# Delta rule in 128-token chunks, its steps emitted between dense products, in a two-block network on one core

## Chip, cores and metric

The kernel runs on one core of a Trainium2 chip. The metric is device time in microseconds (us) of one execution, lower is better. Each time below is from the profiler's record of one execution or from timed runs of the whole kernel.

## What is computed

A two-layer network on 256 latent and 256 context tokens (width 1024) is followed by a second block of two layers on the 256 latent tokens. Only the second block's mixer is touched. It runs a gated delta rule over 8 heads of width 128 beside a sliding-window attention, and gates and sums the two. The reference does the delta rule in chunks of 64 tokens:

```python
def gated_delta_rule_chunked(q, k, v, g, beta):          # C = 64
    gc = cumsum(g) in each chunk
    decay = exp(where(tri_incl, gc[i] - gc[j], -inf))
    L = where(tri_strict, (k * beta) @ k.T * decay, 0)
    A = L + eye(C)
    u, w = solve(A, [v * beta, k * beta * exp(gc)])      # unit lower triangular
    qk = (q @ k.T) * decay
    def step(S, ...):
        v_new = u - w @ S
        o = (q * exp(gc)) @ S + qk @ v_new
        S = S * exp(g_last) + (k * exp(g_last - gc)).T @ v_new
```

The chunk length is a choice of the algorithm: with chunks of 128 the same outputs come from two chunks instead of four.

## The kernel before

All dense products split each float32 operand into a high and a low part and add three products (lines L189 to L191, `mm3`). Weights come in tiles of 512 KB: the SP queue loads `raw` (L177), ScalarE casts `whi` (L181), and VectorE or, for one tile in `pool_every`, GpSimd subtracts `wlo` (L183). Four buffers of each kind run ahead of TensorE.

`mixer2` writes the work of one mixer in program order; a scheduler then fixes the order on each engine by that order and by its own estimates of readiness. On the chip each engine runs its list in order. `Delta` holds the delta rule. Heads go in pairs `pr` (0 to 3); a pair has four blocks `u` (2 heads x 2 halves of 128 tokens).

- `first_keys`, `conv_silu`: projection, short convolution and silu of keys, queries and values, mixed with the dense products.
- `gates`: decay sums (L1672, L1676), written to DRAM so that `rows` can broadcast them.
- `keys`: transposes (L1738), the decay table `W` (L1754 to L1756), the links `LT` = k k^T times `W`, in 64x64 chunks (`chunks`, L1640), written to DRAM.
- `inverse`: 16x16 diagonal blocks are inverted on GpSimd in 15 dependent steps (L1777, L1779), and come back through DRAM as `inv`.
- `levels`: the 16-blocks are joined to 32 and to 64 with small products (L1640), two pairs at a time, and `wT` is made (L1816).
- `queries` and `values`: the table q k^T times decay, again in `chunks`, and the scaled values in `kf`.
- `recur`: four chunk steps (`tb`, `ch`); in each, for two groups `g` of four heads, R·kf (L1861) and wT·S (L1863) are added into one bank, k^T·vk makes the state update (L1871), and W·vt (L1873) and q·S (L1875) are added into the output bank.
- `turn`: transposes of the result (L1904) and their split.

The mixer emits them as whole calls: `keys` for all pairs, `inverse`, `queries`, `levels`, `values`, the z product (512 columns at a time), `recur`, then the gates `yb`, the attention's output product, the gates `ga`, `turn`. A float32 product is two instructions on TensorE: a listing of the order counts products, the trace counts instructions.

Of the kernel before, what the change touches and what calls it, by code (L numbers as in the profile page):

```python
# [19 lines left out]
P = 128  # L20
# [8 lines left out]
def _consts():  # L29
# [67 lines left out]
class Net:  # L97
# [184 lines left out]
    def setup(self):  # L282
# [6 lines left out]
        self.half = self.t(self.cp, [P, 16], tag="half")  # L289
# [989 lines left out]
    def setup2(self, cp):  # L1279
# [6 lines left out]
                      for nm, src, w in (("sgq", "swa_q_norm", 64), ("sgk", "swa_k_norm", 64), ("ssink", "swa_sinks", 16),  # L1286
                                         ("alog", "dn_a_log", 8), ("dtb", "dn_dt_bias", 8))} for l in range(2)]
# [51 lines left out]
    def mixer2(self, x, M, l):  # L1339
# [8 lines left out]
        def gates(dst, c0):  # L1348
            for fb in range(4):
                for _, pa in self.fm_pair(h, 256, w, c0 + fb * 256):  # L1350
                    nc.scalar.activation(dst[:, 2 * fb:2 * fb + 2], pa, AF.Tanh, scale=0.5)

        with pool("mx") as op, ExitStack() as ds:
# [7 lines left out]
            with pool("sw") as ap, pool("inv", side="right") as vp:  # L1361
# [16 lines left out]
                next(swa)  # L1378
                next(swa)
                next(swa)  # L1380
                for pr in range(4):
                    dn.keys(pr)
                dn.inverse(vp)
                dn.queries(0)
                dn.queries(1)
                dn.queries(2)
                dn.queries(3)
                for prs in ((0, 1), (2, 3)):
                    dn.levels(vp, prs)
                next(swa)  # L1390
                dn.values(0)
                next(swa)
                dn.values(1)
                next(swa)
                dn.values(2)
                dn.values(3)
                self.pool_every = 4
# [5 lines left out]
            gain = self.bcast_rows(dp, I["dn_norm_2"][l], P, "dgain")  # L1403
            nc.vector.tensor_scalar(gain, gain, 0.5, None, ALU.mult)
            for hf in range(2):
                def ev_z(tb, pa, hf=hf):
                    g = gz[tb][:, hf * 512:hf * 512 + 512].rearrange("p (h d) -> p h d", d=P)
# [3 lines left out]
                    nc.gpsimd.tensor_tensor(g, g, gain.unsqueeze(1).to_broadcast([P, 4, P]), ALU.mult)  # L1411
                self.proj_tm(h, TBS, w, Z + hf * 512, 512, ev_z)
            with pool("rec") as rp:
                ys = dn.recur(rp, gz)
                gates(yb, GB)
                ws = I["w_swa_out_2"][l]
                with pool("ys", side="right") as yp:
                    ysh, ysl = (self.t(yp, [P, 8, 256], F32R, tag=nm) for nm in ("ysh", "ysl"))
                    for k in (0, 4):
                        for s in (slice(0, P), slice(P, 256)):  # L1420
                            self.split(ysh[:, k:k + 4, s], ysl[:, k:k + 4, s], yT[:, k:k + 4, s])
                    for j in range(4):
                        for _, pa in self.fm_pair(self.flat(ysh, ysl), 256, ws, j * 256):
                            c = yb[:, 2 * j:2 * j + 2]
# [178 lines left out]
class Delta:  # L1603
# [127 lines left out]
    def keys(self, pr):  # L1731
        net, nc, u3, u4 = self.net, self.nc, self.u3, self.u4
        kf, kT, W, LT = self.kf[pr], self.kT[pr], self.W[pr], self.LT[pr]
        if pr > 1:
            self.conv_silu(1024, pr, kf)
# [206 lines left out]
```

## Time and profile before

| | us |
|---|---|
| median of 3 runs | 2421.25 (2411.98 to 2422.31) |
| profiled execution, device time | 2422.13 |
| its span, first to last instruction | 2420.2 |
| TensorE busy in the span | 2305.9 |
| VectorE / ScalarE / GpSimd busy | 1613.3 / 1063.9 / 756.3 |
| mean granted TensorE clock | 0.980 |

How to read it: the first delta stage runs at about 1335 to 1600 us (mixer of layer 0), the second at about 1890 to 2170 us (layer 1). PE is TensorE, DVE VectorE, ACT ScalarE, POOL GpSimd, SP the DMA queue. A timeline row has start, duration, engine, line, operation, out<-in, tile rows*columns, moving shape, count, and in brackets the idle time before it. Matmuls overlap, so what one costs is read from the start of one row to the start of the next. A window row has the stretch, its length, the busy time of PE, PE weight loads, DVE, ACT and POOL with instruction counts, the granted clock (1 is 2.4 GHz, 0.5 is 1.2 GHz), the DMA share and GB/s.

### The profile page before, as it was taken

To read this page: it belongs to the slowest core of one execution; us is meant where nothing else is said; L and a number is where in the kernel's file an instruction comes from. 1 tells how busy PE (TensorE), PEld (TensorE's weight loads), DVE (VectorE), ACT (ScalarE), POOL (GpSimd) and SP (SyncE) were. 2 spreads that over 40 slices of the span, in tenths; PEclk is the share of its full clock that TensorE was granted. 3 is DMA by queue.
4 is the path that set the end of the run, shared out by engine and by line. 5 is a ranking of instruction groups with operands and counts; after the bars stand their busy time and mean duration, and the time that the engine had idled before them with its cause. 6 is when DMAs were issued, how large, how long until landed. Compare 5 with 4: busy or idle time off the path is not lost.

```text
span 2420.2 us, 41624 instructions
## 1 busy us (share of the span) xinstructions
PE 2305.9 (95%) x16388; PEld 2017.7 (83%) x16388; DVE 1613.3 (67%) x2607; ACT 1063.9 (44%) x1748; POOL 756.3 (31%) x545
## 2 busy tenths in 40 slices
PE   6989989999999999988999999999999999999999
PEld 5767667777778788888998888799998887789999
DVE  2677858776566947488647886358766887448773
ACT  3555434332234533345445654245445564345443
POOL 1454421111013122123444662123224572114111
PEclk8989999999999999999999999999999899999999
DMA  7433335476666647477755543255655543245554
GB/s 240 148 105 106 126 111 164 154 227 211 203 203 190 202 154 244 133 242 227 233 180 155 160 115 107 70 157 159 190 183 159 163 120 103 74 139 174 167 183 140
DMA packets 348585, 394.64 MB, mean 163 GB/s; under 512 B 38269, under 2 KB 290093, under 8 KB 346341
## 3 DMA queue, kind: packets, MB, share of 16 engines
q1 hardware_dynamic: 346212, 391.86, 52.5%
q8 instruction: 128, 2.10, 0.4%
q14 instruction: 69, 0.56, 0.1%
q10 hardware_dynamic: 2176, 0.13, 0.1%
HBM read 389.27 MB, written 2.65 MB: 162 GB/s over the span
## 4 chain that ended last, share of the span: by engine, by line
PE 76%; DVE 11%; DMA 6%; issue 3%; POOL 2%; ACT 1%; SPq 1%; DVEq 0%; POOLq 0%; ACTq 0%
PE acc L191 21%; PE acc L190 21%; PE acc L189 21%; DMA mraw<-in_w_ada_dram 2%; DVE macc L383 2%; DVE wlo L183 1%; PE rc L1640 1%; DVE nt L619 1%; DVE hTl L621 1%; PE sm L1873 1%; PE rc L1861 1%; DMA mbig<-in_mod_w_dram 1%; DMA raw<-in_even_w_in_dram 1%; PE sm L1875 1%; PE rc L1863 1%
## 5 line engine op out<-in xcount | busy, mean ns | idle before, releaser
L181 ACT CAST whi<-raw 128x1024 fp32r<-128x1024 f32 (+2 forms) x536 | 552.5, 1033 | 603.1 <-PE acc L190 416.6
L183 POOL TENSOR_TENSOR wlo<-raw,whi 128x1024 fp32r<-128x1024 f32 (+1 forms) x168 | 411.8, 2451 | 1091.3 <-ACT whi L181 1006.7
L189 PE MATMUL acc<-hTh,whi 128*128 128x256 f32 (+2 forms) x2256 | 690.3, 308 | 14.4 <-DVE nu L601 7.9
L190 PE MATMUL acc<-hTl,whi 128*128 128x256 f32 (+2 forms) x2256 | 694.9, 308 | 7.9 <-DVE hTl L621 7.9
L191 PE MATMUL acc<-hTh,wlo 128*128 128x256 f32 (+2 forms) x2256 | 693.8, 308 | 0.7 <-DVE wlo L183 0.7
L183 DVE TENSOR_TENSOR wlo<-raw,whi 128x1024 fp32r<-128x1024 f32 (+1 forms) x368 | 481.0, 1308 | 306.2 <-ACT whi L181 299.8
L189 PEld LDWEIGHTS acc<-hTh,whi 128*128 128x128 f32 x2256 | 429.7, 191 | 46.6 <-issue 12.5
L190 PEld LDWEIGHTS acc<-hTl,whi 128*128 128x128 f32 x2256 | 430.0, 191 | 31.8 <-DVE hTl L621 10.2
L191 PEld LDWEIGHTS acc<-hTh,wlo 128*128 128x128 f32 x2256 | 429.9, 191 | 23.4 <-issue 2.0
L383 DVE SCALAR_TENSOR_TENSOR macc<-mraw,sil,macc 128x512 f32<-128x512 f32 x280 | 247.7, 894 | 82.2 <-DMA mraw<-in_w_ada_dram 43.0
L190 PE MATMUL acc<-hidl,whi 128*128 128x256 f32 (+1 forms) x704 | 218.1, 310 | 0.0
L191 PE MATMUL acc<-hidh,wlo 128*128 128x256 f32 (+1 forms) x704 | 217.7, 310 | 0.0
L189 PE MATMUL acc<-hidh,whi 128*128 128x256 f32 (+1 forms) x704 | 217.6, 310 | 0.0
L189 PE MATMUL acc<-whi,hTh 128*128 128x512 f32 (+2 forms) x496 | 182.4, 370 | 7.5 <-DVE pre L1708 2.8
L190 PE MATMUL acc<-wlo,hTh 128*128 128x512 f32 (+2 forms) x496 | 180.2, 364 | 2.7 <-POOL wlo L183 2.6
L191 PE MATMUL acc<-whi,hTl 128*128 128x512 f32 (+2 forms) x496 | 175.9, 366 | 2.9 <-DVE hTl L621 2.2
L189 PEld LDWEIGHTS acc<-hidh,whi 128*128 128x128 f32 x704 | 132.2, 188 | 9.7 <-issue 1.7
L191 PEld LDWEIGHTS acc<-hidh,wlo 128*128 128x128 f32 x704 | 132.6, 188 | 7.9
L190 PEld LDWEIGHTS acc<-hidl,whi 128*128 128x128 f32 x704 | 132.6, 188 | 7.9
L189 PEld LDWEIGHTS acc<-whi,hTh 128*128 128x128 f32 x496 | 95.1, 192 | 31.3 <-issue 8.4
L191 PEld LDWEIGHTS acc<-whi,hTl 128*128 128x128 f32 x496 | 93.6, 191 | 20.4 <-DVE hTl L621 4.5
L190 PEld LDWEIGHTS acc<-wlo,hTh 128*128 128x128 f32 x496 | 94.9, 191 | 18.0 <-POOL wlo L183 3.1
(531 smaller groups left out, 3829.1 us busy)
## 6 DMA issues: line engine op xcount, KB each, us to landing
raw<-in_w_in_dram SPq DMA_DIRECT2D x112, 512.0 KB
mraw<-in_w_ada_dram SPq DMA_DIRECT2D x192, 256.0 KB
raw<-in_ffn_w_in_dram SPq DMA_DIRECT2D x88, 512.0 KB
raw<-in_w_up_dram SPq DMA_DIRECT2D x88, 512.0 KB
mraw<-in_mod_w_dram SPq DMA_DIRECT2D x96, 256.0 KB
raw<-in_odd_w_in_dram SPq DMA_DIRECT2D x48, 512.0 KB
raw<-in_ffn_w_out_dram SPq DMA_DIRECT2D x40, 512.0 KB
raw<-in_w_down_dram SPq DMA_DIRECT2D x40, 512.0 KB
```

The source lines that it names most:

```text
L181: nc.scalar.copy(hi, raw)
L183: eng.tensor_tensor(lo, raw, hi.bitcast(F32), ALU.subtract)
L189: mm(out, lhsT=ah, rhs=bh, start=start, stop=False)
L190: mm(out, lhsT=ah, rhs=bl, start=False, stop=False)
L191: last = mm(out, lhsT=al, rhs=bh, start=False, stop=stop)
L383: nc.vector.scalar_tensor_tensor(accs[g, m], raw, v[:, k:k + 1], accs[g, m], ALU.mult, ALU.add)
L619: nc.vector.scalar_tensor_tensor(t, x[:, k], a, self.nrs[:, m * 256:m * 256 + 256], ALU.mult, ALU.mult)
L621: nc.vector.scalar_tensor_tensor(lo[:, k, c], t, b, hi[:, k, c].bitcast(F32), ALU.add, ALU.subtract)
L1640: self.nc.tensor.matmul(out[s, u * 64:u * 64 + 64], lhsT=l(u, s), rhs=r(u, s), start=True, stop=True)
L1861: mm(pv[r, s], lhsT=self.R[pr][r, u], rhs=self.kf[pr][r, u], start=True, stop=first)
L1863: mm(pv[r, s], lhsT=self.wT[pr][:, u, r], rhs=S[g][:, i], start=False, stop=True)
L1873: mm(po[g][r, s], lhsT=self.W[pr][r, u], rhs=vt[g][r, i], start=True, stop=first)
```

## The change

Chunks become 128 tokens long, so `W`, `LT` and `R` are 128x128 blocks and the recurrence has two steps in place of four. The products of links and queries are whole 128x128 blocks (`blocks`). `levels` gets one more join, from 64 to 128: the upper 64-block and lower 64-block are inverted as before and their lower-left corner is filled by two more products, which lie in one quarter of the array (`mm`); it works on all four pairs at once with eight `yield` points. `recur` loses the state scaling. `mixer2` calls these steps one by one between convolutions, z products (now 256 columns at a time), gates and the attention's output; `turn` now stands ahead of the last gate piece. The gain of `dn_norm` is loaded early, once.

```diff
-    c["d_min"] = np.where(r6 <= q6, 0.0, NEG).astype(np.float32)
-    c["tri"] = f(same & (r <= q))
-    c["blk"] = f(same)
+    c["d_min"] = np.where(r <= q, 0.0, NEG).astype(np.float32)
+    c["tri"] = f(r <= q)
...
                 sq(0, 0)
                 self.proj_tm(h, TBS, w, 0, 272, ev_k, rows=kab)
+                dn.gates()
                 sq(512, 0)
-                dn.gates()
                 heads = self.swa_heads(ap, sraw, l)
                 swa = self.swa(ap, sraw, heads, yT)
+                dn.keys(0)
+                dn.conv_silu(1024, 2, dn.kf[2])
                 next(swa)
+                dn.links(0)
+                dn.keys(1)
...
+                dn.links(3)
                 dn.inverse(vp)
                 dn.queries(0)
+                dn.conv_silu(0, 2, dn.q[2])
+                next(swa)
...
+                lev = dn.levels(lp)
+                next(lev)
+                dn.first_values(3)
+                dn.values(2)
                 self.pool_every = 4
+                next(lev)
+                z(0)
+                dn.values(3)
+                for f in (lambda: z(1), lambda: z(2), lambda: z(3), lambda: gate(yb, GB, 0), lambda: gate(yb, GB, 1)):
+                    next(lev)
+                    f()
+                for _ in lev:
+                    pass
...
+                next(rec)
+                gate(yb, GB, 3)
+                for j in range(4):
+                    next(rec, None)
+                    for _, pa in self.fm_pair(self.flat(ysh, ysl), 256, ws, j * 256):
...
+                for j in range(3):
+                    gate(ga, GA, j)
                 yd = dn.turn(ys)
+                gate(ga, GA, 3)
...
+    def blocks(self, out, l, r):
+
+        for u in range(4):
+            self.nc.tensor.matmul(out[:, u * P:u * P + P], lhsT=l[:, u], rhs=r[:, u], start=True, stop=True)
+        return self.u3(out)
...
+    def links(self, pr):
+
+        net, nc, kf, LT, W = self.net, self.nc, self.kf[pr], self.LT[pr], self.W[pr]
+        nc.vector.tensor_tensor(LT, self.blocks(net.rc(), kf, kf), W, ALU.mult)
+        nc.sync.dma_start(self.ldram[:, pr * 512:pr * 512 + 512], LT.rearrange("p u t -> p (u t)"))
...
+        def mm(pr, rows, l, r):
+
+            out = bank(pr)
+            for u in range(4):
+                nc.tensor.matmul(out[rows, u * 64:u * 64 + 64], lhsT=l(u), rhs=r(u), start=True, stop=True)
+            return self.uc(out)[rows]
...
+        up, low = halves
         for b in (16, 32):
             for pr in prs:
+                nc.vector.tensor_tensor(Y[pr], lt4(pr), lv(f"lev{b}"), ALU.mult)
+            yield
+            for pr in prs:
+                if b < 32:
+                    nc.vector.tensor_tensor(Tm[pr], Tm[pr], mm4(pr, R[pr], Y[pr]), ALU.subtract)
+                else:
+                    nc.vector.tensor_tensor(Tm[pr][up], Tm[pr][up], mm(pr, up, lambda u: R[pr][up, u], lambda u: Y[pr][up, u]), ALU.subtract)
+            yield
+            for pr in prs:
+                nc.vector.tensor_tensor(R[pr], R[pr], mm4(pr, Y[pr], R[pr]), ALU.subtract)
...
+            nc.scalar.copy(Y[pr][low], mm(pr, low, lambda u: LT[pr][up, u, low], lambda u: Tm[pr][up, u]))
+        yield
+        for pr in prs:
+            for s in halves:
+                nc.gpsimd.tensor_copy(F[pr][s, :, s], R[pr][s])
+            nc.vector.tensor_scalar(F[pr][up, :, low], mm(pr, up, lambda u: Y[pr][low, u], lambda u: R[pr][low, u]), -1.0, None, ALU.mult)
+        yield
...
+                for i, pr, u, s in hds[g]:
+                    mm(pv[:, s], lhsT=self.R[pr][:, u], rhs=self.kf[pr][:, u], start=True, stop=tb == 0)
+                    if tb:
+                        mm(pv[:, s], lhsT=self.wT[pr][:, u], rhs=S[g][:, i], start=False, stop=True)
...
+            yield
+            if tb == 0:
+                for g in range(2):
+                    px = net.rc()
+                    for i, pr, u, s in hds[g]:
+                        mm(px[:, s], lhsT=self.kT[pr][:, u], rhs=vk[g][:, i], start=True, stop=True)
+                    nc.vector.tensor_copy(S[g], self.u3(px))
```

The order of instructions on TensorE at three places of layer 0's mixer follows (rows: line, operation, out<-in, output rows x columns, products). The first is the recurrence; before, in its second chunk step (`acc` rows are dense gate products):

```order
L190 MATMUL acc_15068<-hTl_10417,whi_15058 128x256
L191 MATMUL acc_15068<-hTh_10416,wlo_15059 128x256
L1871 MATMUL rc_14712<-vk_2526_14685,kT_2116_12240 128x128 x2
L1871 MATMUL rc_14712<-vk_2526_14685,kT_2117_12241 128x128 x2
L1873 MATMUL sm_14687<-vt_2524_14683,W_2128_12252 64x128 x2
L1873 MATMUL sm_14687<-vt_2524_14683,W_2129_12253 64x128 x2
L1861 MATMUL rc_14722<-kf_2110_12234,R_2134_12258 64x128
L1863 MATMUL rc_14722<-S_2521_14680,wT_2118_12242 64x128
```

Products there have 64 output rows, and R·kf alternates with wT·S. In the changed kernel the corresponding step takes whole blocks, both head groups at once:

```order
L190 MATMUL acc_15059<-hTh_10420,wlo_15056 128x256
L1923 MATMUL rc_15109<-vk_2566_15031,kT_2115_12241 128x128 x2
L1923 MATMUL rc_15109<-vk_2566_15031,kT_2116_12242 128x128 x2
L1923 MATMUL rc_15115<-vk_2567_15032,kT_2117_12243 128x128 x2
L1923 MATMUL rc_15115<-vk_2567_15032,kT_2118_12244 128x128 x2
L1928 MATMUL sm_15121<-vt_2564_15029,W_2127_12253 128x128 x2
L1928 MATMUL sm_15121<-vt_2564_15029,W_2128_12254 128x128 x2
L1928 MATMUL sm_15122<-vt_2565_15030,W_2129_12255 128x128 x2
L1928 MATMUL sm_15122<-vt_2565_15030,W_2130_12256 128x128 x2
L188 MATMUL acc_15171<-ysh_15017,whi_15161 128x256
```

It stands between two runs of 48 dense instructions each, and so does every step of the new recurrence. The second place is the levels; before, two pairs at a time, with attention and value work close behind:

```order
L1640 MATMUL rc_13816<-T_2376_13748,LT_2130_12254 64x64 x8
L1640 MATMUL rc_13826<-T_2377_13749,LT_2131_12255 64x64 x8
L1544 MATMUL mod_14322<-spT_14308,sraw_2179_12485 64x256 x2
L1544 MATMUL mod_14322<-spT_14309,sraw_2180_12486 64x256 x2
L1844 MATMUL sm_14401<-k_ident_79,tmp_14328 128x128 x4
L1844 MATMUL sm_14480<-k_ident_79,tmp_14407 128x128 x4
```

In the changed kernel all four pairs follow each other, and the new one-quarter products (L1835) come behind:

```order
L1679 MATMUL sm_14705<-R_2453_14143,Y_2449_14139 64x64 x8
L1679 MATMUL rc_14715<-R_2454_14144,Y_2450_14140 64x64 x8
L1679 MATMUL sm_14725<-R_2455_14145,Y_2451_14141 64x64 x8
L1835 MATMUL rc_14735<-T_2444_14134,LT_2131_12257 64x64 x4
L188 MATMUL acc_14771<-hTh_10420,whi_14761 128x256
L189 MATMUL acc_14771<-hTl_10421,whi_14761 128x256
L1835 MATMUL sm_14741<-T_2445_14135,LT_2132_12258 64x64 x4
```

Each level's stage now has 16 or 32 products at a time, with dense products between most stages. The third place is `turn`; before, its 16 transposes stand together, right behind the last gate product:

```order
L191 MATMUL acc_15640<-hTh_10416,wlo_15637 128x256
L1904 MATMUL sm_15698<-k_ident_79,pre_14780 128x128 x4
L1904 MATMUL sm_15707<-k_ident_79,pre_14794 128x128 x4
L1904 MATMUL sm_15716<-k_ident_79,vt_2560_14906 128x128 x4
L1904 MATMUL sm_15725<-k_ident_79,vt_2565_14920 128x128 x4
L189 MATMUL acc_15755<-kT_2655_15690,whi_15745 128x256
```

In the changed kernel the first eight stand ahead of 45 dense instructions of the last gate piece, and the other eight near its end:

```order
L190 MATMUL acc_15717<-hTh_10420,wlo_15714 128x256
L1955 MATMUL sm_15687<-k_ident_79,vt_2612_15325 128x128 x4
L1955 MATMUL sm_15696<-k_ident_79,vt_2617_15339 128x128 x4
L188 MATMUL acc_15717<-hTh_10420,whi_15713 128x256
L189 MATMUL acc_15717<-hTl_10421,whi_15713 128x256
```

So dense work now lies between the two halves of the transposes. Over both mixers, TensorE goes from whole-array work to products on part of the array 92 times before and 61 times in the changed kernel, counted in the two orders from the decay sums on.

## Rows read from the trace of the kernel before

**Rows 1.** The page: busy time, share of the span and instructions of each engine.
```profile
PE 2305.9 (95%) x16388; PEld 2017.7 (83%) x16388; DVE 1613.3 (67%) x2607; ACT 1063.9 (44%) x1748; POOL 756.3 (31%) x545
```

**Rows 2.** Busy time by stretch: keys to levels, recurrence, a feed-forward stretch.
```profile
1335.00:1490.00 155.00, 146.05 (x1394) 127.96 (x1393) 127.80 (x275) 83.46 (x178) 90.02 (x75) 1.00 0.47 128
1490.00:1570.00 80.00, 80.00 (x552) 60.74 (x551) 30.62 (x55) 25.30 (x37) 11.04 (x6) 1.00 0.24 74
...
1700.00:1850.00 150.00, 150.00 (x1270) 150.00 (x1269) 96.24 (x119) 68.42 (x84) 39.80 (x20) 1.00 0.61 187
```

**Rows 3.** Waits of PE, 1335 to 1620 us: total, times, longest.
```profile
PE sm L1904 <- DVE q L168: 3.6, 1, 3.6
...
PE rc L1640 <- DVE T L1799: 1.3, 1, 1.3
```

**Rows 4.** The same view, 1890 to 2180 us.
```profile
PE sm L1904 <- DVE q L168: 2.4, 1, 2.4
```

**Rows 5.** Groups by line, PE: the recurrence's products (busy us, mean ns).
```profile
L1873 PE MATMUL sm<-vt,W 64*64 64x128 f32 x128 | 24.9, 290 | 0.0
L1861 PE MATMUL rc<-kf,R 64*64 64x128 f32 x128 | 24.8, 289 | 0.0
L1875 PE MATMUL sm<-S,q 128*64 128x128 f32 x96 | 20.8, 298 | 0.0
L1863 PE MATMUL rc<-S,wT 128*64 128x128 f32 x96 | 20.8, 298 | 0.0
...
L1871 PE MATMUL rc<-vk,kT 64*128 64x128 f32 x96 | 13.9, 285 | 0.0
```

**Rows 6.** Timeline of PE: whole blocks, then 64-row products, then dense.
```profile
1493.22 1.06 PE L1816 MATMUL rc<-full,kT 128*128 128x128 f32 x8
1494.21 1.08 PE L1861 MATMUL rc<-kf,R 64*64 64x128 f32 x8
1495.22 0.39 PE L189 MATMUL acc<-hTh,whi 128*128 128x256 f32 x1
1495.44 0.29 PE L190 MATMUL acc<-hTl,whi 128*128 128x256 f32 x1
```

**Rows 7.** Timeline of PE: dense, then a 64-row product; further on, the alternation.
```profile
1498.43 0.28 PE L191 MATMUL acc<-hTh,wlo 128*128 128x256 f32 x1
1498.64 1.16 PE L1871 MATMUL rc<-vk,kT 64*128 64x128 f32 x8
...
1508.02 0.43 PE L1863 MATMUL rc<-S,wT 128*64 128x128 f32 x2
1508.38 0.43 PE L1861 MATMUL rc<-kf,R 64*64 64x128 f32 x2
```

**Rows 8.** Timeline of PE: one stage of the levels, two pairs.
```profile
1443.44 1.15 PE L1640 MATMUL rc<-Y,R 64*64 64x64 f32 x32
1444.52 0.50 PE L1510 MATMUL sm<-swmask,identr 128*128 128x512 f32 x1
```

**Rows 9.** Timeline of PE: the links of one pair in 64-column halves.
```profile
1908.01 0.69 PE L1640 MATMUL rc<-kf 128*64 128x64 f32 x16
1908.62 0.66 PE L1738 MATMUL rc<-k_ident,kf 128*128 128x128 f32 x4
```

**Rows 10.** Windows: busy time and clock behind the wait in `turn`.
```profile
1604.00:1611.00 7.00, 5.21 (x25) 5.23 (x26) 3.47 (x9) 2.10 (x6) 0.00 (x0) 0.52 0.52 150
```

**Rows 11.** Groups by line, DVE, 1300 to 1620 us: a 512- and a 256-wide product.
```profile
L1845 DVE TENSOR_TENSOR kf<-sm,dsq 128x512 f32<-128x512 f32 x4 | 2.6, 679 | 0.0
...
L1759 DVE TENSOR_TENSOR LT<-rc,W 128x256 f32<-128x256 f32 x4 | 1.6, 412 | 0.0
```

**Rows 12.** Timeline of POOL: first and last step of the block inverse.
```profile
1397.90 0.22 POOL L1777 TENSOR_TENSOR T<-Y,Y 128x15 f32<-128x15 f32 x1 [1.49 <-DMA tmp<-gdram]
...
1429.99 0.62 POOL L1780 COPY Y<-Y 128x256 f32<-128x256 f32 x1
```

**Rows 13.** Timeline of PE: the first product of the levels.
```profile
1437.17 1.15 PE L1640 MATMUL rc<-T,LT 64*64 64x64 f32 x32 [1.27 <-DVE T L1799]
```

More of the change, by code (lines that the diff above doesn't have):

```diff
@@ L1346, in mixer2 @@
         h = self.fm_tiles()[1]
[L1348 to L1351, printed above, removed]
         with pool("mx") as op, ExitStack() as ds:
@@ L1410, in ev_z @@
                     nc.vector.scalar_tensor_tensor(g, g, 1.0, pz, ALU.add, ALU.mult)
[L1411 to L1415, printed above, removed]
-                ws = I["w_swa_out_2"][l]
[L1417 to L1424, printed above, removed]
-                            nc.vector.scalar_tensor_tensor(c, c, 1.0, pa, ALU.add, ALU.mult)
-                gates(ga, GA)
+                    nc.gpsimd.tensor_tensor(g, g, gain.unsqueeze(1).to_broadcast([P, 2, P]), ALU.mult)
@@ new lines, in z, with gate @@
+                self.proj_tm(h, TBS, w, Z + i * 256, 256, ev_z)
+            def gate(dst, c0, i):
+                for _, pa in self.fm_pair(h, 256, w, c0 + i * 256):
+                    nc.scalar.activation(dst[:, 2 * i:2 * i + 2], pa, AF.Tanh, scale=0.5)
+            with pool("lv") as lp:
+                dn.first_values(2)
+                dn.values(1)
+                lev = dn.levels(lp)
+                next(lev)
+                dn.first_values(3)
+                dn.values(2)
+                self.pool_every = 4
+                next(lev)
[6 more added lines that the diff above has]
+                    pass
@@ new lines, in mixer2 @@
+            vs.close()
+            gate(yb, GB, 2)
+            ys = []
+            with pool("rec") as rp, pool("ys", side="right") as yp:
+                rec = dn.recur(rp, gz, ys)
+                ws = I["w_swa_out_2"][l]
+                ysh, ysl = (self.t(yp, [P, 8, 256], F32R, tag=nm) for nm in ("ysh", "ysl"))
+                for k in (0, 4):
+                    for s in (slice(0, P), slice(P, 256)):
+                        self.split(ysh[:, k:k + 4, s], ysl[:, k:k + 4, s], yT[:, k:k + 4, s])
+                next(rec)
[3 more added lines that the diff above has]
+                    for _, pa in self.fm_pair(self.flat(ysh, ysl), 256, ws, j * 256):
+                        c = yb[:, 2 * j:2 * j + 2]
+                        nc.vector.scalar_tensor_tensor(c, c, 1.0, pa, ALU.add, ALU.mult)
+                for j in range(3):
+                    gate(ga, GA, j)
@@ L1748, in keys @@
         nc.vector.tensor_tensor(kd, tj, self.pr8("k1", pr), ALU.mult)
-        for c in range(2):
-            self.rows(W[c * 64:c * 64 + 64], 0, pr, c * 64)
+        self.rows(W, 0, pr, 0)
         for u in range(4):
@@ new lines, in recur @@
+            yield
+            if tb == 0:
+                for g in range(2):
+                    px = net.rc()
+                    for i, pr, u, s in hds[g]:
+                        mm(px[:, s], lhsT=self.kT[pr][:, u], rhs=vk[g][:, i], start=True, stop=True)
+                    nc.vector.tensor_copy(S[g], self.u3(px))
+            po = [net.sm() for g in range(2)]
+            for g in range(2):
+                for i, pr, u, s in hds[g]:
+                    mm(po[g][:, s], lhsT=self.W[pr][:, u], rhs=vt[g][:, i], start=True, stop=tb == 0)
+                    if tb:
+                        mm(po[g][:, s], lhsT=self.q[pr][:, u], rhs=S[g][:, i], start=False, stop=True)
```

149 lines of the change are left out of this document (57 added, 92 removed).

## The prediction

> **What bounds it now.** I read the page first: TensorE is busy for 95% of the span, VectorE for 67%, ScalarE for 44%, GpSimd for 31% [rows 1]. An average can hide a stage with another bound, so next come the windows. Where keys, inverse and levels are made, TensorE is busy for 146.05 of 155 us; in the recurrence it is never idle, 80.00 of 80 us, while VectorE works 30.62 and the DMA share is 0.24; in a feed-forward stretch with dense products alone it is busy for 150 of 150 us, with VectorE at 96.24 and DMA at 0.61 [rows 2]. The last one matters in two ways. It prices a dense instruction, 150 / 1270 = 0.118 us, and it shows that weights can be loaded, cast and split at the full dense rate. So in the recurrence dense products are not short of weights: they take turns with small products on a full engine. The waits of TensorE confirm it: in the first delta stage the longest is 3.6 us at `turn`, then 1.3 us at the first level [rows 3]; in the second `turn` again, 2.4 us [rows 4]. The kernel is bound by the time that TensorE spends on its list, and what the change is worth is the cost of the small products in that list.
>
> **The recurrence.** One float32 product is two instructions. In both layers before there are 128 of R·kf, 128 of W·vt, 96 each of wT·S, q·S and k^T·vk [rows 5]; half of that per layer. The durations in that view overlap, so I price from start to start. A run of eight R·kf takes 1495.22 - 1494.21 = 1.01 us, 0.126 each; eight whole-block instructions before it take 1494.21 - 1493.22 = 0.99 us, 0.124 each [rows 6]. A 64x64 product is as dear as a 128x128 one. Where 64-row R·kf alternates with 128-row wT·S, two instructions take 1508.38 - 1508.02 = 0.36 us, 0.18 each [rows 7]. W·vt with q·S has the same shapes and gets the same price. Per layer: 16 + 16 instructions of the first chunk, which have no state, and 48 of k^T·vk at 0.126 make 10.1; 4 x 48 = 192 alternating ones at 0.18 make 34.6; together 44.7 us, 89.3 for two layers.
>
> After, per layer, there are R·kf 16, k^T·vk 8, W·vt 16, wT·S 8, q·S 8 products, 56, so 112 instructions, all 128x128, at 0.124: 13.9 us, 27.8 for two. **Saved: 61.5 us.** The state's scaling on VectorE goes too; it was hidden behind TensorE and counts nothing.
>
> **Turns between whole array and part of it.** The dense instruction ahead of a 64-row run starts 1498.64 - 1498.43 = 0.21 us before it [rows 7], and the first dense one behind a run takes 1495.44 - 1495.22 = 0.22 [rows 6], each against 0.118. One excursion costs 0.19 beside its products. There are 92 before and 61 after: 31 x 0.19, **5.9 saved.**
>
> **Levels.** Before, 160 products per layer. After there are 208: the 64-level adds 16 products that keep to one quarter, the 128-join 32 more. That is 96 instructions more per layer, 192 in all. A stage of 32 instructions on two opposite quarters takes 1444.52 - 1443.44 = 1.08 us, 0.034 each [rows 8]; that is the lower bound, since the new ones have no partner. The upper one is R·kf, alone on one quarter with 128 moving columns, 0.126 [rows 6]. I take half of it, 0.063, because the new ones move 64 columns: **12.1 added** (6.5 to 24). VectorE and ScalarE evacuate four pairs per stage instead of two, behind 24 to 48 dense instructions (2.8 to 5.7 us at 0.118), against 4 x 0.412 us [rows 11] for the four.
>
> **Links and queries.** A pair's links took 16 instructions in 1908.62 - 1908.01 = 0.61 us, since two 64-column halves of the array work together [rows 9]. After it is 8 whole blocks, 8 x 0.124 = 0.99. Query products have the same shapes. 4 pairs x 2 x 2 layers x 0.38: **6.1 added.** The Trainium skill (TensorEngine Tiling (Array Packing), Theoretical Speedup) speaks against this edit more sharply: a dimension of 64 gives up to a factor of 2 when tiles share the array. By it whole blocks would cost 2 x 0.61, so 9.8 added instead of 6.1, and the total would be 3.7 us later; the trace has 1.6 between 0.61 and 0.99, and no run yet shows a whole-block link product itself.
>
> **Small edits.** The decay sums lose 4 products per layer, 16 instructions at 0.124: 2.0 saved. The z product in 256-column pieces has the same columns in 192 instructions instead of 96 per layer. Its columns alone take 256 / 2.4 GHz = 0.107 us, so at most 0.011 us per added instruction, 2.1 for both layers, and nothing if the overhead grows with columns; I take 1.0 added. VectorE's link and query multiplications widen from 256 to 512 columns, 0.412 to 0.679 us [rows 11], 16 of them: 4.3 us of VectorE, and the broadcasts and exponentials of `W` double too; SP issues fewer broadcast DMAs of more bytes. I cost these at nothing since TensorE's list covers them; without that cover it is their full length, which goes into a rival.
>
> On TensorE's list: -61.5 - 5.9 + 12.1 + 6.1 - 2.0 + 1.0 = -50.2.
>
> **Waits.** `turn` now has the last gate piece between its halves: 45 dense instructions, 5.3 us, against splits that kept TensorE waiting 3.6 and 2.4 us [rows 3, 4]. Both waits go: -6.0. Behind the first, the granted clock is 0.52 for 7 us, nearly the lower level, 1.2 GHz, after the engine had stood still [rows 10]; 7 x 0.48 = 3.4 us come back. Against that, every stage of the levels hands over to VectorE: 16 handovers in two layers. If a quarter of them wait the 1.3 us that one waited before [rows 3], it is 5.0 added. The rest of the waits I leave.
>
> **Sum:** 2422.1 - 50.2 - 6.0 - 3.4 + 5.0 = 2367.5 on the profiled execution's own device time. It lies 0.9 above the median of the runs, so 2366.6; I say **2367**. With the bounds of the levels and with no or all handovers waiting, this case alone runs from 2356 to 2390.
>
> **Rivals.** *More comes back* (0.14): the new products cost 0.034, no handover waits, and VectorE's lighter recurrence ends some other wait: 2366.6 - 5.6 - 5.0 - 4 = 2352. For it: the opposite quarters of a neighbouring pair may overlap. Against: the quarter products of one pair all lie in the same quarter.
>
> *Waits take back half* (0.16): between 1335 and 1490 VectorE is busy 127.80 of 155 us [rows 2], and it gets wider multiplications there; if all 16 level handovers and the 8 of the recurrence wait 1.3 us, the 5.0 become 31: 2393. Against: 48 dense instructions (5.7 us) stand between the recurrence's steps.
>
> *No gain* (0.06): the dense products cannot close up because their weights come no faster than now. The window of the recurrence moves only 74 GB/s [rows 2], so after the cut it would need the 187 of the feed-forward stretch. If weights held the rate, only waits at `turn` would go: 2421.3 - 6 = 2415. The feed-forward stretch speaks against it.
>
> *Slower* (0.04): the inverse lies bare. Its steps on GpSimd run from 1397.90 to 1430.61 [rows 12], and the first level product starts at 1437.17 [rows 13]: 39 us of latency, of which TensorE saw 1.3. If GpSimd or SP, whose wider `W` products and blocked DMAs are queued ahead of it, delayed it so that each layer waited all 39 us, it would be 2367 - 3 + 78 = 2442. It turns into a loss from 27 us of waiting per layer. Against: after, all queries, two value projections and the whole attention stand between the last links and the first level.
>
> **How the numbers follow.** The likeliest case has 0.60 and gives 2367. Cases above and below it have 0.26 and 0.14. The range **2346 to 2400** takes in the levels' and handovers' bounds, the better rival and the one at 2393, and leaves out no gain, loss, and the tails. 0.5% is 12 us, about what a measurement of this kernel can tell from no change: below 2409 is faster, the first three cases, 0.90; within 12 us is no gain, 0.06; slower 0.04.
>
> **What will show it.** Right: the recurrence's five lines fall to 224 instructions at 0.124 from start to start, with the recurrence's stage some 31 us shorter per layer and still without idle time; the quarter products near 0.063; no wait at `turn` and no low clock behind it. Wrong: new waits of TensorE on VectorE at the levels over 1.3 us each; a wait of tens of us at the first level product; dense instructions starting further apart than 0.118 with waits on `wlo` or `whi`; whole-block products above 0.124, since their addition into one bank is not in the trace before.

## The result and the profile after

The changed kernel takes 2381.97 us in the median (2377.75 to 2387.45), the kernel before 2421.78 in the same runs: a ratio of 0.9843, 95% interval 0.9807 to 0.9878. Timed again later it took 2381.25, ratio 0.9849 (0.9821 to 0.9876). The direction and the range were right; the gain is 40 us where 55 were worked out. The profiled execution, the fastest of its four, has a span of 2375.9 against 2420.2, 44.3 less.

The page of the changed kernel, busy time by engine (beside [rows 1]):

```profile
PE 2258.2 (95%) x16308; PEld 2018.6 (85%) x16308; DVE 1612.3 (68%) x2583; ACT 1064.4 (45%) x1754; POOL 761.3 (32%) x565
```

TensorE is busy for 47.7 us less, and the span fell by less than that: some idle time was added. To place it I cut both traces at the norm's sums ahead of and behind each mixer. Windows of the kernel before, mixer of layer 0 and of layer 1:

```profile
1299.80:1663.60 363.80, 348.97 (x2865) 306.29 (x2864) 248.66 (x457) 177.22 (x323) 151.44 (x112) 0.99 0.44 128
1860.80:2227.50 366.70, 353.00 (x2841) 307.96 (x2840) 249.40 (x455) 177.31 (x322) 148.27 (x112) 0.97 0.44 127
```

The same of the changed kernel:

```profile
1297.10:1645.20 348.10, 329.23 (x2824) 308.88 (x2823) 250.98 (x444) 178.11 (x326) 153.21 (x122) 0.97 0.47 137
1842.80:2181.80 339.00, 322.94 (x2799) 304.11 (x2799) 240.35 (x442) 177.40 (x325) 151.72 (x122) 0.98 0.48 140
```

The two mixers take 687.1 us instead of 730.5, 43.4 of the 44.3. Length less busy time of TensorE is its idle time: 28.5 before, 34.9 after. The column behind the engines is the granted clock; the clock's records, summed, have 27.3 us at 0.50 before and 34.2 after. TensorE is busy for 25.9 and 27.6 us of these stretches, and half of that counts as lost, 13.0 and 13.8. What is left is TensorE's list at full clock: 730.5 - 28.5 - 13.0 = 689.0 before, 687.1 - 34.9 - 13.8 = 638.4 after. All kernels told of here, by this account (sums over two mixers, us; the median is of the whole kernel, the rest of one profiled execution; e1 to e12 are the experiments below):

| kernel | median | mixers | idle | lost to low clock | list |
|---|---|---|---|---|---|
| before | 2421.8 | 730.5 | 28.5 | 13.0 | 689.0 |
| changed | 2382.0 | 687.1 | 34.9 | 13.8 | 638.4 |
| e1 gates late | 2377.6 | 685.9 | 30.5 | 17.2 | 638.2 |
| e2 gates back | 2379.7 | 690.9 | 33.9 | 21.8 | 635.2 |
| e3 old calls | 2383.3 | 685.7 | 39.6 | 12.6 | 633.5 |
| e4 turn back | 2397.0 | 702.1 | 45.2 | 19.0 | 637.9 |
| e5 before, grouped | 2403.4 | 709.5 | 28.1 | 13.4 | 668.0 |
| e6 gates late, layer 0 | 2374.6 | 679.4 | 26.5 | 15.7 | 637.2 |
| e7 old calls, turn | 2371.1 | 678.8 | 32.9 | 11.3 | 634.6 |
| e8 lows on VectorE | 2364.2 | 670.0 | 22.6 | 10.9 | 636.5 |
| e9 = e7 with e8's edit | 2352.1 | 659.7 | 21.4 | 5.4 | 632.9 |
| e10 before, lows on VectorE | 2407.9 | 714.2 | 17.8 | 8.5 | 687.9 |
| e11 = e6 with e8's edit | 2371.2 | 679.5 | 27.9 | 15.5 | 636.1 |
| e12 changed again | 2381.3 | 684.9 | 34.6 | 11.1 | 639.2 |

The waits of TensorE in the changed kernel, layer 0 and then layer 1 (total, times, longest; beside [rows 3, 4]):

```profile
PE sm L1513 <- ACT spT L1510: 7.7, 1, 7.7
PE sm L1530 <- ACT sP L1555: 3.5, 1, 3.5
...
PE sm L1513 <- ACT spT L1510: 6.8, 1, 6.8
PE acc L190 <- DVE wlo L182: 2.4, 1, 2.4
```

`turn` is in neither list any more, and no level waits over 0.3 us. In its place stands L1513, the transposes of the attention's keys. They read `spT`, ScalarE's copy of the keys that VectorE rotates; `pre` in other waits is the short convolution's sum. In the kernel before the same instruction waited for

```profile
PE sm L1480 <- ACT spT L1477: 0.6, 1, 0.6
PE sm L1480 <- ACT spT L1477: 1.0, 1, 1.0
```

The window around the first of them, and the one of the low clock in it:

```profile
1354.00:1376.00 22.00, 13.14 (x79) 11.42 (x77) 21.04 (x56) 10.09 (x22) 6.89 (x5) 0.69 0.41 120
1359.50:1373.00 13.50, 9.24 (x45) 7.74 (x46) 12.69 (x29) 4.95 (x11) 1.58 (x2) 0.50 0.41 126
```

VectorE works for 21.04 of 22 us while TensorE works for 13.14; then the clock is at its lower level, 1.2 GHz, for 13.5 us, after TensorE had stood still since 1354.9. This is the wait that the prediction did not have. The 2.4 at `wlo` in layer 1 is a smaller one of the kind that it named as a sign of being wrong.

The recurrence's products of the changed kernel, by line (busy us, mean ns; beside [rows 5]), and its timeline where R·kf and wT·S alternate (beside [rows 7]):

```profile
L1928 PE MATMUL sm<-vt,W 128*128 128x128 f32 x64 | 10.1, 275 | 0.0
L1911 PE MATMUL rc<-kf,LT 128*128 128x128 f32 x64 | 10.1, 275 | 0.0
...
L1913 PE MATMUL rc<-S,wT 128*128 128x128 f32 x32 | 6.2, 275 | 0.0
L1930 PE MATMUL sm<-S,q 128*128 128x128 f32 x32 | 6.2, 275 | 0.0
...
L1923 PE MATMUL rc<-vk,kT 128*128 128x128 f32 x32 | 3.9, 275 | 0.0
```

```profile
1540.64 0.38 PE L1911 MATMUL rc<-kf,LT 128*128 128x128 f32 x2
1540.86 0.39 PE L1913 MATMUL rc<-S,wT 128*128 128x128 f32 x2
...
1543.10 0.39 PE L1913 MATMUL rc<-S,wT 128*128 128x128 f32 x2
```

The lines have 224 instructions in all. From 1540.64 to 1543.10 there are 22 of them, 0.112 each, with no more for the alternation; over both layers they take 24.3 us from start to start, 0.109 each. The new quarter products, alone on their quarter (beside [rows 8]):

```profile
1488.22 0.68 PE L1835 MATMUL rc<-Y,R 64*64 64x64 f32 x8
...
1489.67 0.63 PE L1835 MATMUL sm<-Y,R 64*64 64x64 f32 x8
1490.23 0.38 PE L188 MATMUL acc<-whi,hTh 128*128 128x256 f32 x1
```

32 in 1490.23 - 1488.22 = 2.01 us, 0.063 each, as taken.

### The profile page after: what moved, and what is told of

Same layout as the page of the kernel before. It is cut to its first block, busy times and chain, and to the rows that moved or that the text cites. A ratio compares the mean times of both kernels' runs of the same rounds, so it can differ in the third digit from the quotient of the medians.

```text
span 2375.9 us, 41450 instructions
## 1 busy us (share of the span) xinstructions
PE 2258.2 (95%) x16308; PEld 2018.6 (85%) x16308; DVE 1612.3 (68%) x2583; ACT 1064.4 (45%) x1754; POOL 761.3 (32%) x565
## 5 line engine op out<-in xcount | busy, mean ns | idle before, releaser
L188 PE MATMUL acc<-hTh,whi 128*128 128x256 f32 (+2 forms) x2256 | 693.0, 309 | 13.4 <-DVE nu L600 8.0
L188 PE MATMUL acc<-whi,hTh 128*128 128x512 f32 (+2 forms) x560 | 193.6, 347 | 6.8 <-DVE nu L600 2.2
L189 PE MATMUL acc<-wlo,hTh 128*128 128x512 f32 (+2 forms) x560 | 190.3, 341 | 2.7 <-POOL wlo L182 2.6
L190 PE MATMUL acc<-whi,hTl 128*128 128x512 f32 (+2 forms) x560 | 186.8, 343 | 2.8 <-DVE hTl L620 2.2
L188 PEld LDWEIGHTS acc<-whi,hTh 128*128 128x128 f32 x560 | 107.2, 192 | 28.2 <-issue 8.1
L190 PEld LDWEIGHTS acc<-whi,hTl 128*128 128x128 f32 x560 | 105.8, 191 | 18.7 <-DVE hTl L620 4.4
L189 PEld LDWEIGHTS acc<-wlo,hTh 128*128 128x128 f32 x560 | 107.0, 191 | 15.6 <-POOL wlo L182 3.1
```

Of the source, the lines that this page charges most:

```text
L188: mm(out, lhsT=ah, rhs=bh, start=start, stop=False)
L189: mm(out, lhsT=ah, rhs=bl, start=False, stop=False)
L190: last = mm(out, lhsT=al, rhs=bh, start=False, stop=stop)
```

## Experiments

**e1: the order on VectorE.** In the changed kernel VectorE has 16 subtractions on the decay table `W` (L1785), of all four pairs, ahead of the last key rotations. First theory: this order makes the wait for `spT`.

```diff
-                dn.gates()
                 sq(512, 0)
...
-                dn.keys(0)
                 dn.conv_silu(1024, 2, dn.kf[2])
+                dn.gates()
+                dn.keys(0)
```

> The changed kernel with one call moved: gates, which releases the subtractions of the decay table W on VectorE, stands behind the attention's heads and the convolution of pair 2 instead of ahead of the second query projection. Theory A (order on VectorE): TensorE waits 7.7 and 6.8 us for spT because the 16 instructions on W stand ahead of the key rotations in VectorE's list. With the rotations ahead, these two waits fall under 1.5 us each, and the low clock behind the first (13.7 us at half speed) goes: 2375.9 - 13 - 6 = a span of 2357, 2353 to 2364. Rival B (amount of work): VectorE has too much to do in that stretch whatever the order; the waits reappear at another consumer and the span stays at 2372 to 2379.

2377.57 us, ratio 0.9806 (0.9783 to 0.9828). Layer 0 does as theory A says: its mixer falls from 348.1 to 340.2 us, and the longest wait left there is 2.8. Layer 1 does as B says: 345.7 against 339.0, with waits of 3.0 at `pre`, 2.7 at `wlo`, 2.2 at `dneg` and 10.2 us more of low clock. The theory in its full form falls, but in layer 0 the order makes the wait.

**e2: `gates` behind the second query projection alone.**

```diff
-                dn.gates()
                 sq(512, 0)
+                dn.gates()
```

> The changed kernel with gates moved only behind the second query projection, which is where the kernel before has it. The listing still has 12 to 16 of the instructions on W ahead of the last key rotation. Theory A (order on VectorE): the waits for spT stay mostly, 4 to 8 us each, span 2368 to 2376. Rival C (the place of gates against that projection is what matters, by the extra 48 dense instructions it gives VectorE): both waits fall under 2 us, span 2355 to 2364.

2379.65 us, 0.9817 (0.9795 to 0.9839); 690.9 us in the mixers. In layer 0 the wait for `spT` stays, 6.4 us, so the place against the projection is not what matters there. In layer 1 it goes and 4.2 at `pre` comes; the span, 2380.5, lies above both theories. One engine in order, full for a stretch, lets someone wait; the order decides who.

**e3: the chunk length without the new emission.** `Delta` as changed, in a mixer that calls the steps whole.

```diff
+                for pr in range(4):
+                    if pr > 1:
+                        dn.conv_silu(1024, pr, dn.kf[pr])
+                    dn.keys(pr)
+                    dn.links(pr)
                 dn.inverse(vp)
...
+                for _ in dn.levels(lp):
                     pass
+            z(0)
+            z(1)
...
+                for _ in dn.recur(rp, gz, ys):
+                    pass
```

> Chunks of 128 tokens as in the changed kernel, but steps emitted as whole calls in the order of the kernel before: three attention steps, keys and links of all pairs, inverse, queries, values between attention steps, then all levels at once (behind the attention, since their tiles don't fit beside it), z in 512 columns, the whole recurrence, gates, attention's output product, gates, turn. Theory A: nearly all of the gain is the chunk length, on TensorE's list (65 us in the recurrence), and does not need the new emission; what the emission gave is the wait at turn (6 us) and a low clock (3.4 us), what it cost is the wait at spT (13 us): span 2365 to 2390. Rival D: without dense products between them the levels and the two steps of the recurrence wait for VectorE at each of 24 handovers, 1.3 us or more each, and more than 30 us come back: span over 2400.

2383.33 us, 0.9835 (0.9816 to 0.9854), theory A. The gain comes from the chunk length; all of the emission together earned nothing that can be measured. The list is 633.5 against 638.4, the waits at `turn` are back (3.6 and 2.4), and no product of the levels or the recurrence waits over 1.0 us although nothing was written between them: the scheduler puts dense products between the recurrence's steps by itself, and in the levels the four pairs cover for each other. The wait for `spT` is there too, 6.3 in layer 0, so there it does not come from the new emission.

**e4: `turn` behind the last gate piece.**

```diff
-                for j in range(3):
+                for j in range(4):
                     gate(ga, GA, j)
                 yd = dn.turn(ys)
-                gate(ga, GA, 3)
```

> The changed kernel with turn behind the last piece of the gates ga instead of ahead of it. Theory A: the two waits of the kernel before return, 3.6 and 2.4 us, and with the first the low clock of some 7 us, so 6 to 9.5 us more: span 2382 to 2385. Rival E: in the changed kernel the recurrence ends so early that its normalisation is ready anyway, the splits are all that is waited for, and TensorE loses under 3 us: span 2374 to 2379.

2396.98 us, 0.9889 (0.9869 to 0.991): 15 us of the gain lie on one line, more than theory A gave. The two waits come back exactly (3.6 and 2.4), and a low clock of 3.4 us behind each. The rest, 4 us of idle time in both layers and 7 us more of low clock in layer 1, lies ahead of `turn`. In layer 0, where VectorE's order is that of the changed kernel, the mixer grows by 4.9 us; in layer 1 it grows by 10.1, and there the orders on TensorE and VectorE change with the edit too, so that part is not shown to be `turn`'s own.

**e5: what made the old recurrence dear.** The kernel before, with its alternating products grouped.

```diff
                     for i, pr, u, s in hds:
-                        mm(pv[r, s], lhsT=self.R[pr][r, u], rhs=self.kf[pr][r, u], start=True, stop=first)
-                        if not first:
-                            mm(pv[r, s], lhsT=self.wT[pr][:, u, r], rhs=S[g][:, i], start=False, stop=True)
+                        mm(pv[r, s], lhsT=self.R[pr][r, u], rhs=self.kf[pr][r, u], start=True, stop=True)
+                    if not first:
+                        for i, pr, u, s in hds:
+                            mm(pv[r, s], lhsT=self.wT[pr][:, u, r], rhs=S[g][:, i], start=True, stop=True)
...
```

W·vt and q·S are edited the same way.

> The kernel before (64-token chunks), with the recurrence's products grouped: four R·kf and then four wT·S, and four W·vt and then four q·S, in place of the alternation. The second four overwrite the bank in place of adding to it (the addition of R·kf and W·vt is left out); count, shapes and order around them are the same. Theory A (the alternation of 64-row and 128-row products is what costs 0.18 instead of 0.126 each): 192 alternating instructions per layer save 0.054 each, 20.7 us in two layers, less some 24 changes of shape at 0.05, so the four lines take 55 to 58 us from start to start instead of 76.4 and the time falls to 2402 to 2404. Rival B (the price belongs to products that add into a bank just written, or to state columns as operands): the products keep 0.16 to 0.18 and the time stays within 4 us of before.

2403.39 us, 0.9921 (0.9892 to 0.9951). The four lines take 55.0 us from start to start instead of 76.4, 0.119 to 0.126 an instruction. Theory A by its numbers: the alternation cost 21 us, a third of what the change saves in the recurrence. The edit takes away two things at once, though, the alternation and the adding into one bank. That the adding has no price of its own is argued from the changed kernel, where whole blocks add into one bank at 0.112 (above); no run has 64-row products that add without alternating. In the profile by line the same products, each shorter than in [rows 5]:

```profile
L1861 PE MATMUL rc<-kf,R 64*64 64x128 f32 x128 | 17.2, 275 | 0.0
L1874 PE MATMUL sm<-vt,W 64*64 64x128 f32 x128 | 17.2, 275 | 0.0
...
L1877 PE MATMUL sm<-S,q 128*64 128x128 f32 x96 | 13.1, 279 | 0.0
L1864 PE MATMUL rc<-S,wT 128*64 128x128 f32 x96 | 12.9, 278 | 0.0
```

**e6: e1's order in layer 0 alone.**

> The changed kernel with gates behind the convolution of pair 2 (as in e1) in layer 0 alone; layer 1 as in the changed kernel. Theory A (in layer 0 the order on VectorE makes the wait; in layer 1 other consumers stand in line): layer 0's mixer takes 340 us as in e1 against 348, layer 1's 339 against 346 in e1, so the span is 2366 to 2371. Rival B (both differences are scatter of single executions): the two mixers sum to 684 to 690 again, span 2374 to 2381.

2374.63 us, 0.9813 (0.9779 to 0.9846). The mixers take 340.3 and 339.1, and the span of 2370.1 lies in theory A's range. That the mixers agree to the microsecond is partly luck: the four executions run from 2368.75 to 2379.96. In layer 1 the orders are those of the changed kernel and the time is the same; in layer 0 they are e1's, and so is the time. The median gains 7 us on the changed kernel's, which the intervals don't separate.

**e7: e3 with `turn` ahead of the last gate piece.**

```diff
-                for j in range(4):
+                for j in range(3):
                     gate(ga, GA, j)
                 yd = dn.turn(ys)
+                gate(ga, GA, 3)
```

> The kernel of e3 (128-token chunks, steps as whole calls), with turn ahead of the last piece of the gates ga. Theory A: the waits of 3.6 and 2.4 us at turn go, and the low clock behind each (3.4 us at half speed) with them, so 6 to 9.5 us less than e3: mixers of 676 to 680 against 685.7, span 2372 to 2377, earlier than the changed kernel. Rival B: what the place of turn is worth depends on the emission around it; by e4 it was 15 us, so the mixers would come to 671.

2371.14 us, 0.9798 (0.9776 to 0.9821). Theory A by the profile (678.8, 6.9 less than e3); the medians differ by 12. The orders ahead of `turn` hardly change here, so this is the cleaner price of its place. With `turn` alone in the new place, whole calls are some 11 us faster than the changed kernel: the rest of the new emission cost about what `turn` earned.

**e8: GpSimd's share of `wlo`.** GpSimd makes every second `wlo` in the key and attention stage. What happens beside it on VectorE in the changed kernel, VectorE's timeline:

```profile
1343.04 3.35 DVE L1785 SCALAR_TENSOR_TENSOR W<-W,dgc,k_main 128x128 f32<-128x128 f32 x4
...
1348.63 1.12 DVE L1785 SCALAR_TENSOR_TENSOR W<-W,dgc,k_main 128x128 f32<-128x128 f32 x4
...
1358.15 0.65 DVE L1792 TENSOR_TENSOR LT<-rc,W 128x512 f32<-128x512 f32 x1
1358.72 1.69 DVE L1504 TENSOR_TENSOR sraw<-sraw,rcos 128x32 f32<-128x32 f32 x2
```

and GpSimd's:

```profile
1343.01 2.40 POOL L182 TENSOR_TENSOR wlo<-raw,whi 128x1024 fp32r<-128x1024 f32 x1
...
1357.69 2.35 POOL L182 TENSOR_TENSOR wlo<-raw,whi 128x1024 fp32r<-128x1024 f32 x1
```

Four subtractions on `W` take 1.12 us away from such a `wlo` and 3.35 when they start beside one; the rotations at 1358.72 end only behind the second one.

```diff
-            self.pool_every = 2
+            self.pool_every = 1000
             for pr in range(2):
                 dn.first_keys(pr, self.rc if pr else self.acc)
```

> The changed kernel with no wlo on GpSimd from the mixer's first key to the levels: VectorE subtracts them all. In the changed kernel GpSimd makes 13 and 15 of them in the two key and attention stages, 2.4 us each, and VectorE instructions that start beside them are stretched, by 21.0 and 17.3 us in sum. Theory A (a VectorE instruction that meets a wlo on GpSimd stands still until it ends, so that GpSimd's share costs VectorE more than it takes off): VectorE gets 28 x 1.2 = 34 us more work and 38 us less stretch, the wait for spT falls by the 2.4 us blocks ahead of it, to 2 to 5 us, and the span falls by 2 to 10 us. Rival B (the stretch is hidden in idle time anyway): VectorE is 34 us busier where it is the bound, and the span grows by 5 us or more.

2364.23 us, 0.9766 (0.9745 to 0.9788), 18 us faster than the changed kernel; the span is 12.4 shorter, above theory A's upper end. Windows of its two mixers:

```profile
1302.60:1640.60 338.00, 324.46 (x2816) 305.56 (x2816) 247.26 (x459) 177.86 (x326) 119.80 (x107) 0.97 0.48 141
1837.80:2169.80 332.00, 322.94 (x2807) 303.50 (x2806) 242.09 (x457) 177.44 (x326) 118.47 (x107) 0.98 0.49 143
```

VectorE makes 30 instructions more (916 for 886), which at 1.21 us are 36 us of work, and is busy for 489.35 us instead of 491.34: the stretches were as long as the work that GpSimd took off it. GpSimd is busy for 66.7 us less. The wait of L1513 is off the list in both layers; 6.5 us at `pre` and 4.2 at the keys' low part are left. The edit does one thing more: the scheduler orders the engines anew by it, and on VectorE only 4 of the 16 subtractions on `W` still stand ahead of the last key rotation. In the changed kernel all 16 do, and that rotation starts at 1362.25. Here it is followed by the subtractions:

```profile
1356.29 0.28 DVE L1506 TENSOR_TENSOR sraw<-sraw,spT 128x128 f32<-128x128 f32 x1
1356.49 0.34 DVE L1785 SCALAR_TENSOR_TENSOR W<-W,dgc,k_main 128x128 f32<-128x128 f32 x1
```

So order and length change together, and how much of the 18 us is due to each is not shown.

**e9: e7 with e8's edit.**

> The kernel of e7 (128-token chunks, whole calls, turn ahead of the last gate piece) with no wlo on GpSimd from the first key until behind the values, as in e8. Theory A (GpSimd's subtractions hold VectorE up in the key and attention stages whatever the emission): the waits for spT and pre of e7 (6.3 and 5.7 us) shrink to half or less, low clock with them, and the mixers fall from 678.8 to 665 to 672 us, span 2356 to 2363, level with e8; then the emission one by one is worth nothing beside turn. Rival B (the steps one by one are what lets VectorE's relief through; whole calls pile up): at most 3 us come off, span 2366 to 2371.

2352.14 us, 0.9721 (0.9699 to 0.9744): faster than both kernels and than e8, and 5 us below theory A's range in the mixers and the span.

```profile
1302.90:1634.80 331.90, 318.91 (x2720) 296.44 (x2719) 247.37 (x455) 177.40 (x322) 120.32 (x103) 0.99 0.47 143
1830.50:2158.30 327.80, 319.37 (x2710) 296.31 (x2709) 238.49 (x453) 177.57 (x322) 117.56 (x103) 0.99 0.47 145
```

Against e8 the idle time is nearly the same (21.4, 22.6); the low clock costs half as much and the list is 3.6 shorter, with 193 instructions less, nearly all of them of z. As in e8, 4 of the 16 subtractions on `W` are left ahead of the last rotation, where e7 has 16.

**e10: the kernel before with e8's edit.**

> The kernel before (64-token chunks) with the same single edit as e8: no wlo on GpSimd in the key, attention and level stages. There 37 of them take 97 us of GpSimd, stretch VectorE by 33.6 us and would cost VectorE 37 x 1.2 = 44 us. Theory A (VectorE became the bound of that stretch only through the change, which puts the wider tables ahead of the attention's keys): TensorE's waits there were short before, so the time moves by less than 4 us, span 2416 to 2424. Rival B (the stretches cost the kernel before just as much): its time falls by 8 us or more, span under 2412.

2407.85 us, 0.9947 (0.9929 to 0.9965): rival B.

```profile
1301.70:1662.90 361.20, 350.43 (x2856) 308.87 (x2856) 250.51 (x472) 178.16 (x323) 112.72 (x97) 0.98 0.43 129
1859.10:2212.10 353.00, 345.96 (x2847) 302.72 (x2846) 248.42 (x471) 177.35 (x323) 111.52 (x97) 1.00 0.43 132
```

Idle time falls from 28.5 to 17.8. VectorE makes 31 instructions more (943 for 912; the expectation had 37) and is busy for 498.93 us in place of 498.05: here too the share moved no work. The edit is worth 14 us to the kernel before as well, in many short waits; the change did not bring the stretches in, it put a long wait behind them. None of the subtractions on `W` stood ahead of the last rotation in layer 0 before, and two in layer 1, but elsewhere the scheduler's order changes here too.

**e11: e6 and e8 together.**

> The changed kernel with both edits: gates late in layer 0 (e6) and no wlo on GpSimd in the key and attention stages (e8). Theory A (the two act on the same wait in layer 0, by order and by length, and a remnant is left in e8: 6.5 us at pre): layer 0's mixer falls below e8's 338.0, to 331 to 336, layer 1's stays at 332, span 2357 to 2362. Rival B (the wait is gone in e8 already, and what is left belongs to the convolutions): 337 to 342 in layer 0, span 2362 to 2368.

2371.18 us, 0.9799 (0.9777 to 0.9822): theory A falls, and it is slower than e8 by 7. Layer 0 takes 343.6 with waits of 4.2 in three pieces (`spT` behind the scores), 3.8 in two (`sP`) and 2.3; layer 1, where the calls stand as in e8, takes 335.9 against 332.0 in another order of the scheduler's. The comparison with e6 says more: in layer 0 both have the rotations ahead of every subtraction on `W`, and there e8's edit brings nothing, 343.6 against 340.3, with 16.8 us of idle time against 12.1. What it is worth depends on the order that comes of it.

**e12: the changed kernel again.**

> The changed kernel itself, for the same runs of the kernel before. If its profile is typical: the two mixers 687 us, 43 less than before, with waits for spT of 6 to 8 us in both layers, median 2376 to 2384. If the waits were scatter of one execution: mixers 672 to 680 and a median near 2367.

348.0 and 336.9 us in the mixers, waits for `spT` of 7.6 and 5.9: its profile was typical.

## Why the prediction was right, and where its sum was off

- **TensorE's list: right, in part by terms that offset each other.** -50.2 forecast, 689.0 to 638.4 = -50.6 measured. With whole calls and e8's edit on both sides (e10 to e9) it is -55.0.
- **The recurrence: mechanism right, price too high.** -61.5 forecast; 89.4 to 24.3 is -65.1, since a whole-block product took 0.109 us in place of 0.124. That the old price held some 0.054 in each of 384 instructions that grouping takes off is shown by e5.
- **Levels: right.** +12.1 forecast; the 192 quarter products take 12.2 us from start to start (0.064 each, no overlap between neighbouring pairs). At full clock all of the levels take 21.9 us before and 34.7 after, +12.8.
- **Links and queries: too high.** +6.1 forecast. Before, all of them took 12.5 us, 1.9 of it at the low clock; after 16.4, 4.1 of it at the low clock. At full clock that is 11.5 and 14.4, and 13.6 in e9: +2.1 to +2.9. Halves were dearer than the pair in [rows 9], 0.045 an instruction against 0.038, and whole blocks cheaper than 0.124, 0.106 in e9. The Trainium skill's factor of up to 2 (TensorEngine Tiling (Array Packing), Theoretical Speedup), by which 9.8 would have been added, does not show here: 16 half-column instructions at 0.045 take 0.72 us, 8 whole blocks at 0.106 take 0.85.
- **Decay sums: right.** -2.0 forecast; 3.4 to 1.6 us is -1.8.
- **Excursions and z: not measured one by one.** The terms above make -65.1 + 12.8 + 2.9 - 1.8 = -51.2, so all the rest together is +0.6, where -4.9 was forecast: no run shows the 5.9 that fewer excursions were to save.
- **`turn`: right.** The waits of 3.6 and 2.4 and the low clock behind them are gone, and e4 brings them back.
- **Handovers of the levels, +5.0: wrong.** The longest is 0.3 us, and 1.0 with whole calls (e3). The upper bounds of the levels and the handovers, added up, give 2394 and not the 2390 of the prediction.
- **The step that failed is "The rest of the waits I leave."** I had taken VectorE's wider instructions as covered by TensorE's list. In the key and attention stage VectorE was not covered: the attention's keys, whose waits were 0.6 and 1.0 us and which I did not look at, waited 7.7 and 6.8. In layer 0 it was VectorE's order that did it: before, the 16 subtractions on `W` stand behind the last key rotation, in the changed kernel ahead of it, and with the rotations ahead again (e1, e6) the wait is gone and the mixer 8 us shorter. Idle time rose by 6.4 where waits were to fall by 1.0 in sum, and the low clock cost 0.8 more where 3.4 were to come back. 6.4 + 1.0 + 0.8 + 3.4 = 11.6 lost; the list was 0.4 better; 54.6 - 11.6 + 0.4 = 43.4, what the mixers show.
- **A reading that might have warned.** The prediction takes "1.3 us at the first level" for the next wait behind `turn`, and `turn` for the longest in layer 1. The same two views of the kernel before have longer ones, both on VectorE, the first in the key stage (1363.04) and the second behind the first level (2008.94):

```profile
PE rc L1738 <- DVE LT L1759: 2.3, 1, 2.3
PE acc L189 <- DVE pre L1708: 2.8, 1, 2.8
```

- **The rival "waits take back half"** had the right engine and stretch (VectorE, 1335 to 1490) and the wrong victim. Its 31 us at the levels and the recurrence did not come.

What makes the wait is shown in part: in layer 0 it goes with the order on VectorE (e1, e6), and in layer 1 another order moves it to other victims (e1, e2). In e8, with no `wlo` on GpSimd, it goes in both layers, but there the order changes too, and with the rotations ahead in both kernels the same edit gained nothing in layer 0 (e6, e11). So what the stretches alone cost stays open. With that edit on both sides, chunks of 128 with `turn` in its new place bring 2407.85 - 2352.14 = 55.7 us (e10 to e9), near the 54.6 forecast; the list is 4.8 us better there than forecast and the idle time grows by 3.6 where it was to fall by 1.0, so the nearness is partly luck. Open too: why the rest of the new emission costs some 11 us (e7 against the changed kernel, e9 against e8). In the account it lies in the list (3.8 and 3.6), the low clock (2.5 and 5.5) and idle time (2.0 and 1.2), with no one wait behind it.

## What to carry to other kernels

When a change packs more into a stage, price the slack of the engine next to the bound there, instruction by instruction in its order, and look at the waits that are short now: the wait that grows need not be at the code that was changed. Shapes that alternate on TensorE can cost nearly half the work again (0.18 us an instruction for 0.126); group them, or make them alike, before a larger rewrite. Before work is shared out to GpSimd, see what VectorE's instructions beside it become: here sharing took no time off VectorE. And where a scheduler fixes the order, look at what an edit did to it before reading its price: an edit that moved only work between engines moved the order on TensorE, VectorE and ScalarE.

## What the runs showed of the hardware

- A VectorE instruction with both tensors in SBUF that started beside a GpSimd subtraction ended only behind it (L1504 at 1358.72 and L1785 at 1343.04, above), while one that reads its first operand from PSUM did not notice (`LT<-rc,W`, 0.65 us beside the same `wlo`). The Trainium skill says so (SBUF — State Buffer, SBUF: two separate sides: of a VectorE instruction with two SBUF inputs and a GpSimd instruction that reads SBUF, the one that starts first holds the shared port pair for its whole length and the other blocks), and the trace agrees. I had not expected that 30 tiles' worth of help, 67 us of GpSimd, would come to nothing on VectorE, nor that taking it back, with the order that came of it, would make kernels 14 to 19 us faster (e10, e8, e9).
- 64-row products that alternate with 128-row ones cost 0.18 us each, in groups of their like 0.12 to 0.126 (e5, where the adding into one bank goes as well); 128x128 products with different operands alternate at 0.112 without any such price.
- The low clock followed idle time of TensorE and outlasted it: 13.5 us at 1.2 GHz, begun within a wait of 7.7. TensorE was busy for 9.24 us of that stretch; with half of that lost, the wait cost 1.6 times its length.
